# Two layers of a hybrid DeltaNet, sliding-window and memory-attention trunk: decay differences from two split passes with a triangle of ones, and two attention steps each one unit later

## The chip, the cores and the metric

The kernel runs on one core of a Trainium2 chip. The metric is device time in microseconds of one execution, the median of several. PE is the TensorE matmul engine, PEld its weight loads, DVE VectorE, ACT ScalarE, POOL GpSimd, SP the queue that issues the weight DMAs.

## The reference, cut to what matters

```python
def hybrid_layer(x, mem_n, ...):
    h = layer_norm(ALPHA * x + 0.5 * swiglu(x, ...))
    (dn_q, dn_k, dn_v, dn_b, dn_a, dn_z, sw_q, sw_k, sw_v, xa_q, gates) = split(h @ w_in)
    o_dn = deltanet_branch(dn_q, dn_k, dn_v, dn_b, dn_a, dn_z, ...)
    o_sw = sliding_window_attention(sw_q, sw_k, sw_v, swa_sinks)
    o_xa = memory_cross_attention(xa_q, mem_n, w_mem_kv)
    merged = sum_n sigmoid(gates_n) * (branch_n @ w_branch_n)
    h = layer_norm(ALPHA * h + merged @ w_out)
    return layer_norm(ALPHA * h + 0.5 * swiglu(h, ...))
```

In the DeltaNet branch g is a log-decay per token and head, and the scores are weighted with the decay between two tokens:

```python
g = cumsum(g)
decay = exp(where(tril, g[..., :, None] - g[..., None, :], NEG_INF))
```

The difference of the two running sums is the sum of g over the tokens after the earlier and up to the later one. There are 256 tokens, two layers, four DeltaNet heads of 128, eight window heads of 64 with a window of 128 tokens and two key/value heads, four memory heads of 128. Everything is float32.

## The kernel before, in words

**Weights** stream from DRAM in one array, in the order of use, as *units* of 128 x 1024 numbers (`unit`, line 103). Each unit is loaded by SP into `raw` (four buffers), cast to `whi` on ACT (a rounded float32, the type that PE takes in one pass), and the rest `raw - whi` goes to `wlo` on DVE (both in `split`, line 125). `whi` and `wlo` have five buffers each, so the cast of a unit waits until PE has read the unit five before it. A float32 product is made of three such matmuls (`mm3`: high x high, high x low, low x high). A matmul of two plain float32 operands is left to PE, which then runs several passes; the trace shows each as two records.

**PSUM** has four banks `acc` for the projections and two each of `at` (attentions) and `sm` (DeltaNet). A bank is handed on in turn, so its next writer waits until all readers of its last content are done.

**Order of the work.** `mixers` (once for each layer) runs the projections of the three branches as a stream of units. `weave` hangs small steps of the attentions and of the DeltaNet behind given units. The instructions of PE stay in program order there (`pinned`). On ACT, DVE and POOL a scheduler chooses the order when the program is built; the queue of each engine then runs in that fixed order, whatever is ready.

The steps that matter here, with their lines:

- `spread(c)` (line 652), for the two blocks c of 128 tokens: POOL has made `TM[c][:,0]`, the triangle `mlt` times g for four heads (line 673); PE multiplies each head's 128 x 128 block with the triangle `tri`, all plain float32, into one `sm` bank; DVE adds the mask (L658), ACT takes the exponential (L659).
- `gates(n)` projects the gates of branch n in eight units; each unit is twelve matmuls of 512 columns, and a tanh (L977) follows the fourth and the eighth. `gates(1)` carries the steps that are moved.
- `w_scores(tb, hh)` makes window scores of 128 tokens and half of the heads: six matmuls into two `at` banks, L736 on DVE (scale and mask), L742 to L746 (maximum), L745 and L748 on ACT (four exponentials), L749 and L750 on DVE, and L751 on ACT, four scalings by one over the sum. `w_turn` transposes the result on PE; ACT and DVE copy it (L761). `w_values(tb)` multiplies it with the values and splits the result.
- `double()` is the next stage of the inversion of two triangular matrices (one for each c), seven stages in all: small matmuls into `sm` for c=0 and then for c=1, and copies back. The copies of stage three are L856, two for each c, all four on ACT.

Of the kernel before, what the change touches and what calls it, by code (L numbers as in the profile page):

```python
# [11 lines left out]
F32R = mybir.dt.float32r  # L12
I32 = mybir.dt.int32
AF = mybir.ActivationFunctionType
ALU = mybir.AluOpType
AX = mybir.AxisListType

P = 128
# [20 lines left out]
def tile_trunk(ctx, tc, x, xT, mem, memT_, wst, lnp, memln, cvw, rows, cst, out):  # L39
    nc = tc.nc  # L40
# [3 lines left out]
    pc = ctx.enter_context(tc.tile_pool(name="pc", bufs=1))  # L44
    praw = ctx.enter_context(tc.tile_pool(name="praw", bufs=4))
    pu = ctx.enter_context(tc.tile_pool(name="pu", bufs=1))
    p2 = ctx.enter_context(tc.tile_pool(name="p2", bufs=2))
# [7 lines left out]
    def nm(s):  # L55
        uid[0] += 1
        return f"{s}_{uid[0]}"
# [4 lines left out]
    def T(pool, shape, tag, dt=F32, bufs=None):  # L62
        pool = pn if pool is pu and tag in NEAR else pool
        kw = {} if bufs is None else {"bufs": bufs}
        return pool.tile(shape, dt, tag=tag, name=nm(tag), **kw)
# [4 lines left out]
    def at():  # L70
        return T(psT, [P, 512], "at")

    def sm():
        return T(psS, [P, 512], "sm")
# [7 lines left out]
    tri = cs[:, C_TRI:C_TRI + P]  # L82
    mlt = cs[:, C_LT:C_LT + P]
    dtm = cs[:, C_DTM:C_DTM + P]

    def over4(ap):
        return ap.unsqueeze(1).to_broadcast([P, 4, ap.shape[-1]])
# [36 lines left out]
    def split(hi, lo, src):  # L124
        return nc.scalar.copy(hi, src).ins, nc.vector.tensor_tensor(lo, src, hi.bitcast(F32), op=ALU.subtract).ins  # L125
# [3 lines left out]
    def pe(ins):  # L129

        return tc.keep_in_program_order(ins) if pinned[0] else ins

    def matmul(*a, **k):
        return pe(nc.tensor.matmul(*a, **k))  # L134
# [10 lines left out]
    def weave(work, steps):  # L145

        for n, _ in enumerate(work, 1):
            for f in steps.get(n, ()):
                f()

    def projB(xt, nt, kpu, behind=None):
        g = projB_parts(xt, nt, kpu, behind)
        while True:
            try:
                next(g)
            except StopIteration as e:
                return e.value

    def projB_parts(xt, nt, kpu, behind=None):
        banks = [acc().rearrange("p (t s) -> p t s", t=2) for _ in range((nt + 1) // 2)]  # L160
        for uu in range(KD // kpu):
            hi, lo = unit(behind=behind)
            for kk in range(kpu):
                k = uu * kpu + kk
                for t in range(nt):
                    c = (kk * nt + t) * P
                    o = banks[t // 2][:, t % 2, :]
                    lastt = t % 2 == 1 or t == nt - 1
                    matmul(o, hi[:, c:c + P], xt[0](k), start=(k == 0 and t % 2 == 0), stop=False, skip_group_check=True)
                    matmul(o, hi[:, c:c + P], xt[1](k), start=False, stop=False, skip_group_check=True)  # L170
                    matmul(o, lo[:, c:c + P], xt[0](k), start=False, stop=(k == KD - 1 and lastt), skip_group_check=True)
            yield
        return banks

    def halves(xt, use):

        for i in range(2):
            (b,) = yield from projB_parts(xt, 2, 4)
            use(i, b)
# [66 lines left out]
    def acc_of(t):  # L246
        return (lambda k: t[0][:, k, :], lambda k: t[1][:, k, :])
# [271 lines left out]
    def mixers(l, hT, mkT, mv_, post):  # L519
        xt = acc_of(hT)  # L520
# [79 lines left out]
        def col(tag):  # L600
            return T(pu, sh, tag)
# [30 lines left out]
        g = col("g")  # L632
# [15 lines left out]
        TM = [T(pu, [P, 2, 4, P], f"w{2 + c}") for c in range(2)]  # L648
        AK = [T(pu, [P, 4, 2, P], f"u{12 + c}") for c in range(2)]
        hb = lambda ap: ap.unsqueeze(2).to_broadcast([P, 4, P])  # L650

        def spread(c):

            gm, dt = TM[c][:, 0], TM[c][:, 1]
            ps = sm().rearrange("p (h c) -> p h c", h=4)
            for h in range(4):
                matmul(ps[:, h, :], gm[:, h, :], tri, start=True, stop=True)
            nc.vector.tensor_tensor(dt, ps, over4(dtm), op=ALU.add)  # L658
            nc.scalar.activation(dt, dt, AF.Exp)  # L659

        def products(c, hh):
# [6 lines left out]
            for j in range(2):  # L668
                h = 2 * hh + j
                nc.vector.scalar_tensor_tensor(AK[c][:, h], TM[c][:, 1][:, h, :].unsqueeze(1).to_broadcast([P, 2, P]), cS[:, c, h:h + 1], ps[:, j], op0=ALU.mult, op1=ALU.mult)  # L670

        for c in range(2):
            nc.gpsimd.tensor_tensor(TM[c][:, 0], over4(mlt), hb(g[:, c, :]), op=ALU.mult)


        xq = (T(pu, [P, 4, S], "u4", F32R), T(pu, [P, 4, S], "u6", F32R))
# [47 lines left out]
        def w_scores(tb, hh):  # L724

            ts = slice(tb * P, (tb + 1) * P)
            nk = P if tb == 0 else 2 * P
            msk = cs[:, C_SW + P:C_SW + 2 * P] if tb == 0 else cs[:, C_SW:C_SW + 2 * P]
            pr = wpr[tb, hh] = T(p2, [P, 4, S], "pp")
            for j in range(0, 2, 2 * P // nk):  # L730

                nj = 2 * P // nk
                ps = at().rearrange("p (j v k) -> p j v k", j=nj, v=2)
                for i in range(nj):
                    mm3(ps[:, i], [t[:, 2 * hh + j + i, ts] for t in sq_], [t[:, :, 0:nk] for t in swk], True, True)
                nc.vector.scalar_tensor_tensor(pr[:, 2 * j:2 * j + 2 * nj, :nk], ps.rearrange("p j v k -> p (j v) k"), 0.125, msk.unsqueeze(1).to_broadcast([P, 2 * nj, nk]), op0=ALU.mult, op1=ALU.add)  # L736
            mxs = T(p3, [P, 2, 2], "mx")
            sums = T(p3, [P, 4], "sums")
            sk = T(p3, [P, 2, 2], "sk")
            sink = sinks[:, 2 * hh:2 * hh + 2, :]  # L740
            flat = lambda t: t.rearrange("p i v -> p (i v)")
            nc.vector.tensor_reduce(flat(mxs), pr[:, :, :nk], axis=AX.X, op=ALU.max)  # L742
            nc.vector.tensor_tensor(mxs, mxs, sink, op=ALU.max)
            nc.vector.tensor_tensor(sk, sink, mxs, op=ALU.subtract)
            nc.scalar.activation(flat(sk), flat(sk), AF.Exp)  # L745
            nc.vector.tensor_scalar(flat(mxs), flat(mxs), -1.0, None, ALU.mult)  # L746
            for h in range(4):
                nc.scalar.activation(pr[:, h, :nk], pr[:, h, :nk], AF.Exp, bias=mxs[:, h // 2, h % 2:h % 2 + 1], accum_out=sums[:, h:h + 1])  # L748
            nc.vector.tensor_tensor(sums, sums, flat(sk), op=ALU.add)  # L749
            wpr["end"] = nc.vector.reciprocal(sums, sums).ins  # L750
            [nc.scalar.mul(pr[:, h, :nk], pr[:, h, :nk], sums[:, h:h + 1]) for h in range(4)]  # L751
# [11 lines left out]
        def w_values(tb):  # L763
            if not oS:
                oS.extend(T(pu, [P, 4, S], tag, F32R) for tag in ("u6", "u7"))
            ts = slice(tb * P, (tb + 1) * P)
            pso = at()
            for kb in range(tb + 1):
                for kv in range(2):
                    hs = slice(kv * 64, kv * 64 + 64)  # L770
                    matmul(pso[hs, :], swv[:, kb, hs], wpT[tb][kb][:, kv].rearrange("p h q -> p (h q)"), start=kb == 0, stop=kb == tb)
            split(oS[0][:, :, ts], oS[1][:, :, ts], pso.rearrange("p (h k) -> p h k", h=4))
# [43 lines left out]
        def use_sq(i, b):  # L816
            split(*(t[:, 2 * i:2 * i + 2, :] for t in sq_), b)

        weave(halves(xt, use_xq), {3: [tok_v]})
        (b,) = projB(xt, 1, 8)  # L820
        for kv in range(2):
            hs = slice(kv * 64, kv * 64 + 64)
# [157 lines left out]
        def branch(n, o):  # L980
# [27 lines left out]
            3: [lambda: w_turn(0, 1), begin_inverse],  # L1008
            4: [lambda: w_scores(1, 0)]})
        weave(gates(1), {  # L1010
            1: [lambda: w_values(0), double],
            2: [lambda: w_scores(1, 1)],
            3: [double],
            5: [double, lambda: w_turn(1, 0)],
            6: [double, lambda: w_turn(1, 1)],
            7: [double, lambda: w_values(1)],
# [56 lines left out]
    ps = sm()  # L1073
# [14 lines left out]
    for l in range(NL):  # L1088
        mT = []
        mid = memory_T(mT, l)  # L1090
        if l == 0:

            mid[2] = lambda: load(cs, cst)
            more = {4: lambda *a: xres(0), 6: lambda *a: xres(1), 8: lambda *a: small()}
        post = Post(lnp[l, 0, 0], lnp[l, 0, 1])
        f1.rest(hT, 4, [((pu, "u0"), (pu, "u1")), ((pu, "u2"), (pu, "u3"))], post, mid, ends, {} if l else more)
        kv = memory_kv(mT, post.end)
        if l == 0:
            nc.scalar.activation(nea, rw[:, :, 8:12], AF.Exp)
            nc.vector.tensor_scalar(nea, nea, -1.0, None, ALU.mult)  # L1100
        post2 = Post(lnp[l, 1, 0], lnp[l, 1, 1])
        mixers(l, post.hT, *kv, post2)
        f2 = Ffn()
        begin(f2, post2.hT)
        last = l == NL - 1
        post = Post(lnp[l, 2, 0], lnp[l, 2, 1], last)
        f2.rest(post2.hT, 6, [((pu, a), (pu, b)) for a, b in (("u0", "u1"), ("u2", "u3"), ("u4", "u5"), ("u6", "u13"))], post, behind=post2.end)
        ends = post.end
        if not last:
            f1, hT = Ffn(), post.hT  # L1110
            begin(f1, hT)
# [87 lines left out]
```

## Time and profile before

| | |
|---|---|
| median of 3 runs | 1274.8 us (1273.62 to 1275.08) |
| profiled execution, its own time | 1273.52 us |
| its span | 1271.7 us |
| PE busy | 1261.0 us (99%) |
| DVE / ACT / POOL busy | 865.5 / 660.7 / 206.7 us (68 / 52 / 16%) |
| mean granted TensorE clock | 0.999 |

The profiled execution's own time is 1.8 us over its span, and 1.3 us under the median. A PE that is busy 99% says that it always has a matmul under way by the profile, not that each runs at its best: ends of matmuls are modelled, and a matmul that starts late shows first in the distance from one start to the next.

### The profile page before, as it was taken

How to read it: one execution, taken by the hardware profiler on the slowest of the kernel's cores; microseconds unless marked ns; L12 is line 12 of the kernel's file. 1: busy time of each engine (PE TensorE's matmuls, PEld its weight loads, DVE VectorE, ACT ScalarE, POOL GpSimd, SP SyncE). 2: the span in 40 equal slices, each digit the busy share in tenths (PEclk: the TensorE clock that was granted, in tenths of full speed). 3: DMA queues.
4: the chain of work that ended last, by engine and by line, in shares of the span. 5: the costliest groups of instructions: out<-in, count | busy, mean ns of one | idle time of the engine just before them, and what ended most of it. 6: DMA issues, size and time to landing. Idle time of an engine off the chain costs nothing.

```text
span 1271.7 us, 18766 instructions
## 1 busy us (share of the span) xinstructions
PE 1261.0 (99%) x6948; PEld 1073.7 (84%) x6948; DVE 865.5 (68%) x1273; ACT 660.7 (52%) x982; POOL 206.7 (16%) x365
## 2 busy tenths in 40 slices
PE   9999999999999999999999999999999999999997
PEld 6888889999878888888888888899987788888886
DVE  6678576897647776665766665759867388666555
ACT  6456444655664544454454554456556554444441
POOL 1232100002311102221012220000023101122200
PEclk9999999999999999999999999999999999999999
DMA  8988765655534748786667886566464356577762
GB/s 301 307 272 281 256 212 158 206 170 134 173 117 145 243 142 257 240 242 220 216 208 245 256 256 214 180 185 212 151 167 134 100 188 226 174 245 245 241 223 81
DMA packets 77499, 261.40 MB, mean 206 GB/s; under 512 B 11904, under 2 KB 13056, under 8 KB 77408
## 3 DMA queue, kind: packets, MB, share of 16 engines
q1 hardware_dynamic: 66320, 232.53, 55.8%
q0 software_dynamic: 11088, 27.68, 8.0%
q8 instruction: 54, 0.88, 0.3%
q14 instruction: 37, 0.30, 0.1%
HBM read 246.40 MB, written 13.76 MB: 205 GB/s over the span
## 4 chain that ended last, share of the span: by engine, by line
PE 96%; DVE 1%; DMA 1%; ACT 1%; issue 0%; SPq 0%; DVEq 0%; ACTq 0%
PE acc L134 85%; PE at L134 4%; PE sm L134 3%; PE sm L137 2%; DMA raw<-in_wst_dram 1%; DVE wlo L125 1%; PE acc L328 1%; PE acc L329 1%; PE acc L331 1%; PE at L137 1%; ACT whi L125 1%; DVE h L291 0%; DVE pp L736 0%; DVE w L940 0%; SPq L115 0%
## 5 line engine op out<-in xcount | busy, mean ns | idle before, releaser
L125 DVE TENSOR_TENSOR wlo<-raw,whi 128x1024 fp32r<-128x1024 f32 (+2 forms) x405 | 489.0, 1214 | 280.1 <-ACT whi L125 277.5
L125 ACT CAST whi<-raw 128x1024 fp32r<-128x1024 f32 (+2 forms) x405 | 413.6, 1029 | 400.1 <-PE acc L134 321.2
L134 PE MATMUL acc<-whi,hT 128*128 128x512 f32 (+1 forms) x1824 | 563.0, 386 | 0.4 <-ACT whi L125 0.4
L134 PEld LDWEIGHTS acc<-whi,hT 128*128 128x128 f32 x1824 | 340.2, 188 | 70.0 <-ACT whi L125 2.1
L134 PE MATMUL acc<-wlo,hT 128*128 128x512 f32 (+1 forms) x912 | 350.3, 384 | 0.0
L134 PE MATMUL acc<-whi,u 128*128 128x512 f32 x812 | 259.7, 392 | 0.0
L134 PEld LDWEIGHTS acc<-wlo,hT 128*128 128x128 f32 x912 | 171.4, 188 | 32.9 <-DVE wlo L125 1.1
L134 PEld LDWEIGHTS acc<-whi,u 128*128 128x128 f32 x812 | 152.3, 188 | 32.2 <-DVE u L125 0.5
L134 PE MATMUL acc<-wlo,u 128*128 128x512 f32 x406 | 158.2, 390 | 0.0
L358 POOL DMA_DIRECT2D tr<-t x176 | 96.2, 553 | 307.9 <-DVE t L352 299.3
L134 PE MATMUL acc<-hT,whi 128*128 128x256 f32 x672 | 122.3, 284 | 0.0
L134 PEld LDWEIGHTS acc<-hT,whi 128*128 128x128 f32 x672 | 104.7, 192 | 0.0
L134 PE MATMUL acc<-hT,wlo 128*128 128x256 f32 x336 | 95.1, 283 | 0.0
L134 PEld LDWEIGHTS acc<-wlo,u 128*128 128x128 f32 x406 | 76.3, 188 | 15.3
L134 PEld LDWEIGHTS acc<-hT,wlo 128*128 128x128 f32 x336 | 64.3, 192 | 0.0
L359 POOL DMA_DIRECT2D pt<-tr x44 | 25.0, 568 | 196.9 <-DMA tr<-t 128.9
L349 ACT ACTIVATE t<-acc 128x256 f32<-128x256 f32 x88 | 33.4, 379 | 36.7 <-PE acc L134 36.6
L134 PE MATMUL acc<-u,u 128*128 128x512 f32 x186 | 46.4, 394 | 0.0
L350 DVE TENSOR_TENSOR t<-t,acc 128x256 f32<-128x256 f32 x88 | 36.6, 416 | 8.0 <-ACT t L349 4.7
L995 POOL TENSOR_TENSOR u<-u,gt 128x512 f32<-128x512 f32 x16 | 20.7, 1294 | 125.0 <-DVE gt L993 125.0
L134 PEld LDWEIGHTS acc<-u,u 128*128 128x128 f32 x186 | 34.6, 188 | 7.5
L125 DVE TENSOR_TENSOR u<-pt,u 128x512 fp32r<-128x512 f32 x44 | 28.9, 657 | 10.3 <-ACT u L125 10.3
(236 smaller groups left out, 1163.7 us busy)
## 6 DMA issues: line engine op xcount, KB each, us to landing
raw<-in_wst_dram SPq DMA_DIRECT2D x409, 512.0 KB, 4.4
tr<-t POOLq DMA_DIRECT2D x176, 64.0 KB, 4.0
pt<-tr POOLq DMA_DIRECT2D x44, 256.0 KB, 5.2
raw<-in_wst_dram SPq DMA_DIRECT2D x16, 324.0 KB, 3.0
gB<-in_lnp_dram SPq DMA_DIRECT2D x6, 512.0 KB, 5.9
bB<-in_lnp_dram SPq DMA_DIRECT2D x6, 512.0 KB, 6.2
w<-dr POOLq DMA_DIRECT2D x4, 512.0 KB, 11.2
t<-in_xT_dram SPq DMA_DIRECT2D x4, 256.0 KB, 5.5
```

Source lines behind the costliest of these rows:

```text
L125: return nc.scalar.copy(hi, src).ins, nc.vector.tensor_tensor(lo, src, hi.bitcast(F32), op=ALU.subtract).ins
L134: return pe(nc.tensor.matmul(*a, **k))
L137: return pe(nc.tensor.transpose(*a))
L328: nc.tensor.matmul(ps, hT[0][:, k, ts], hi[:, c], start=k == 0, stop=False)
L329: nc.tensor.matmul(ps, hT[0][:, k, ts], lo[:, c], start=False, stop=False)
L331: nc.tensor.matmul(ps, hT[1][:, k, ts], hi[:, c], start=False, stop=k == KD - 1)
L349: act = nc.scalar.activation(t[:, :, tb, :], g, AF.Silu).ins
L350: ins = nc.vector.tensor_tensor(t[:, :, tb, :], t[:, :, tb, :], u, op=ALU.mult).ins
L358: nc.gpsimd.dma_start(d[:, :, q].rearrange("b c x -> c b x"), z[32 * q:32 * q + 32].rearrange("c (b x) -> c b x", b=4))
L359: back = nc.gpsimd.dma_start(y, d.rearrange("b c q x -> (b c) (q x)")).ins
L995: nc.gpsimd.tensor_tensor(mg[tb][:, js], mg[tb][:, js], gt[tb][:, js], op=ALU.add)
```

## The change

1. `spread` works with a new constant `later`, the triangle `mlt` cast to the rounded type (exact, it holds ones and zeros), as the stationary operand. The moving operand is now `tri` times g, made by POOL as before and split into a high and a low part by the new `spread_parts` (a cast on ACT and a subtraction on DVE of 128 x 512 for each c) into a tile of the pool that later holds the gates' tanh. Two matmuls of 512 columns, high and low, replace the four plain float32 ones.
2. `spread_parts(0)` and `spread_parts(1)` hang behind the first and third unit of the memory queries' projection.
3. In `gates(1)`, `w_values(0)` goes from behind unit 1 to behind unit 2, and `w_scores(1, 1)` from behind unit 2 to behind unit 3.

```diff
+    later = pc.tile([P, P], F32R, name="later")
...
         def spread(c):
-            gm, dt = TM[c][:, 0], TM[c][:, 1]
+            dt = TM[c][:, 1]
             ps = sm().rearrange("p (h c) -> p h c", h=4)
-            for h in range(4):
-                matmul(ps[:, h, :], gm[:, h, :], tri, start=True, stop=True)
+            for n in range(2):
+                matmul(ps, later, gms[c][n], start=n == 0, stop=n == 1)
...
+        gms = {}
         for c in range(2):
-            nc.gpsimd.tensor_tensor(TM[c][:, 0], over4(mlt), hb(g[:, c, :]), op=ALU.mult)
+            nc.gpsimd.tensor_tensor(TM[c][:, 0], over4(tri), hb(g[:, c, :]), op=ALU.mult)
+
+        def spread_parts(c):
+            both = T(p2, [P, 2, 4, P], "gt", F32R)
+            gms[c] = both[:, 0], both[:, 1]
+            split(*gms[c], TM[c][:, 0])
...
-        weave(halves(xt, use_xq), {3: [tok_v]})
+        weave(halves(xt, use_xq), {1: [lambda: spread_parts(0)], 3: [tok_v, lambda: spread_parts(1)]})
...
         weave(gates(1), {
-            1: [lambda: w_values(0), double],
-            2: [lambda: w_scores(1, 1)],
-            3: [double],
+            1: [double],
+            2: [lambda: w_values(0)],
+            3: [double, lambda: w_scores(1, 1)],
             5: [double, lambda: w_turn(1, 0)],
             6: [double, lambda: w_turn(1, 1)],
...
+            nc.scalar.copy(later, mlt)
             nc.scalar.activation(nea, rw[:, :, 8:12], AF.Exp)
```

New lines shift the numbers of the code behind them: L125 of before is L126 in the order of the change, L134 is L135, L745 to L751 are L753 to L759, L856 is L864, L871 is L879, L977 is L985.

**ACT, behind units 4 to 6 of `gates(1)`, layer 0, before.** The first cast needs the end of unit 4 on PE, the second of unit 5, the third of unit 6; `pp` are the window scores (1, 1), the first `w` copies fill the matrices of stage three.

```order
L745 ACTIVATE sk_3546<-sk_3546 128x4
L125 CAST whi_3828<-raw_3827 128x1024
L748 ACTIVATE pp_3533,sums_3545<-pp_3533,mx_3544 128x256 x4
L125 CAST whi_3834<-raw_3833 128x1024
L751 ACTIVATE pp_3533<-pp_3533,sums_3545 128x256 x4
L977 ACTIVATE gt_3451<-acc_3453 128x512
L856 COPY w_461_2590<-sm_3658 32x4x32 x2
L856 COPY w_462_2591<-sm_3669 32x4x32 x2
L761 COPY pt_3680<-at_3682 128x2x2x128
L125 CAST whi_3840<-raw_3839 128x1024
```

The same place in the changed program:

```order
L126 CAST whi_3832<-raw_3831 128x1024
L985 ACTIVATE gt_3455<-acc_3457 128x512
L126 CAST whi_3838<-raw_3837 128x1024
L753 ACTIVATE sk_3606<-sk_3606 128x4
L756 ACTIVATE pp_3593,sums_3605<-pp_3593,mx_3604 128x256 x4
L864 COPY w_461_2592<-sm_3662 32x4x32 x2
L864 COPY w_462_2593<-sm_3673 32x4x32
L759 ACTIVATE pp_3593<-pp_3593,sums_3605 128x256 x2
L126 CAST whi_3844<-raw_3843 128x1024
L759 ACTIVATE pp_3593<-pp_3593,sums_3605 128x256 x2
L864 COPY w_462_2593<-sm_3673 32x4x32
L769 COPY pt_3684<-at_3686 128x2x2x128
```

The exponentials moved from ahead of the second cast to behind it, and the third cast (`whi_3840`, now `whi_3844`) moved from behind all of this to the middle: two scalings, the fourth copy of stage three and the copy of `w_turn(1, 0)` now stand behind it. Layer 1 has the same two sequences.

**PE, behind units 1 to 3 of `gates(1)`, layer 0, before**, without the projection's own rows: the values (`at` from `pt`), stage one, the scores (1, 1) (`at` from `swk`, the last row of six), stage two.

```order
L134 MATMUL at_3474<-pt_3379,swv_2063 64x512 x2
L134 MATMUL sm_3479<-w_470_2601,l_469_2600 32x32 x16
L134 MATMUL sm_3497<-w_470_2601,l_469_2600 32x32 x16
...
L134 MATMUL at_3539<-swk_99,bB_2599 128x512
...
L134 MATMUL sm_3580<-w_470_2601,w_461_2590 32x32 x16
L134 MATMUL sm_3599<-w_470_2601,w_462_2591 32x32 x16
```

The same in the changed program:

```order
L135 MATMUL sm_3476<-w_470_2603,l_469_2602 32x32 x16
L135 MATMUL sm_3494<-w_470_2603,l_469_2602 32x32 x16
...
L135 MATMUL at_3532<-pt_3383,swv_2065 64x512 x2
...
L135 MATMUL sm_3555<-w_470_2603,w_461_2592 32x32 x16
L135 MATMUL sm_3574<-w_470_2603,w_462_2593 32x32 x16
...
L135 MATMUL at_3599<-swk_100,bB_2601 128x512
```

The values stand alone behind unit 2, and the scores follow stage two directly; stages one and two stay behind units 1 and 3.

## Rows read from the trace of the kernel before

**Rows 1.** The page, busy time of each engine.
```profile
PE 1261.0 (99%) x6948; PEld 1073.7 (84%) x6948; DVE 865.5 (68%) x1273; ACT 660.7 (52%) x982; POOL 206.7 (16%) x365
```
**Rows 2.** Timeline of PE around both spreads (start, us, engine, line, operation, count).
```profile
283.62 0.28 PE L134 MATMUL acc<-hT,wlo 128*128 128x256 f32 x1
...
283.75 1.05 PE L134 MATMUL sm<-cs,w 128*128 128x128 f32 x8
...
284.55 1.66 PE L134 MATMUL at<-u,u 128*128 128x256 f32 x12
...
286.05 0.40 PE L134 MATMUL acc<-hT,whi 128*128 128x256 f32 x2
...
288.81 0.28 PE L134 MATMUL acc<-hT,wlo 128*128 128x256 f32 x1
...
290.06 0.29 PE L134 MATMUL acc<-hT,wlo 128*128 128x256 f32 x1
```
**Rows 3.** Timeline of PE, end of unit 1 of `gates(1)` and the steps behind it.
```profile
341.90 0.39 PE L134 MATMUL acc<-wlo,hT 128*128 128x512 f32 x1
...
342.13 0.39 PE L134 MATMUL acc<-whi,hT 128*128 128x512 f32 x1
...
342.70 1.08 PE L134 MATMUL at<-pt,swv 128*64 128x512 f32 x4 [0.18 <-DVE pp L736]
...
343.70 1.51 PE L134 MATMUL sm<-w,l 32*32 32x32 f32 x64
...
345.14 0.50 PE L134 MATMUL acc<-whi,hT 128*128 128x512 f32 x1
```
**Rows 4.** Timeline of PE, stage two behind unit 3.
```profile
351.94 0.39 PE L134 MATMUL acc<-whi,hT 128*128 128x512 f32 x1
...
352.26 1.51 PE L134 MATMUL sm<-w,w 32*32 32x32 f32 x64
...
353.69 0.50 PE L134 MATMUL acc<-whi,hT 128*128 128x512 f32 x1
```
**Rows 5.** Timeline of PE, last matmuls of units 5 and 6, stage four, `w_turn(1, 1)`.
```profile
359.04 0.39 PE L134 MATMUL acc<-whi,hT 128*128 128x512 f32 x1
...
363.63 0.39 PE L134 MATMUL acc<-whi,hT 128*128 128x512 f32 x1
363.95 0.89 PE L134 MATMUL sm<-w,w 32*32 32x32 f32 x32
364.77 1.09 PE L137 MATMUL at<-cs,pp 128*128 128x128 f32 x8
```
**Rows 6.** Timeline of ACT, the same stretch.
```profile
356.37 0.20 ACT L745 ACTIVATE sk<-sk 128x4 f32<-128x4 f32 x1
...
357.70 0.51 ACT L748 ACTIVATE pp<-pp,mx 128x256 f32<-128x256 f32 x1
...
359.68 1.03 ACT L125 CAST whi<-raw 128x1024 fp32r<-128x1024 f32 x1
360.61 1.71 ACT L751 ACTIVATE pp<-pp,sums 128x256 f32<-128x256 f32 x4
362.22 0.58 ACT L977 ACTIVATE gt<-acc 128x512 f32<-128x512 f32 x1
362.81 1.08 ACT L856 COPY w<-sm 32x128 f32<-32x128 f32 x4
363.92 0.58 ACT L761 COPY pt<-at 128x512 f32<-128x512 f32 x1
```
**Rows 7.** Timeline of PE and ACT, end of unit 7 and the cast that waits for it.
```profile
368.23 0.39 PE L134 MATMUL acc<-whi,hT 128*128 128x512 f32 x1
...
368.65 1.04 ACT L125 CAST whi<-raw 128x1024 fp32r<-128x1024 f32 x1 [0.64 <-PE acc L134]
```
**Rows 8.** The last stretch of the span (busy us of PE, PEld, DVE, ACT, POOL, then PEclk).
```profile
1265.00:1271.00 6.00, 0.00 (x0) 0.00 (x0) 3.25 (x8) 0.21 (x1) 0.00 (x0) 0.83 0.23 87
```
**Rows 9.** Timeline of DVE, the mask of the second spread.
```profile
290.02 0.69 DVE L658 TENSOR_TENSOR w<-sm,cs 128x512 f32<-128x512 f32 x1 [1.43 <-PE sm L134]
```

## The prediction

> **What bounds the kernel now.** I read the page first: PE is busy 99% of the span [rows 1], so almost every microsecond taken from PE's stream, or added to it, reaches the end, and work on ACT, DVE or POOL counts only where PE waits for it. As a late start hides in the modelled ends, I then read the timeline at the places that change, by distances between starts. A step of 256 columns takes 0.12 us (twelve in the 1.50 us from 284.55 to 286.05 [rows 2]), one of 512 columns 0.23 us (341.90 to 342.13 [rows 3]). Then I looked for who waits on whom among PE and ACT in `gates(1)`, since ACT's order is what moves most there [rows 5 to 7]. The casts of units stand behind PE: the one behind unit 7 begins 0.03 us after that unit's last matmul ends (368.23 + 0.39 = 368.62, cast at 368.65 [rows 7]). So all five buffers are full, and a cast is some four units ahead of its use.
>
> **Removed from PE: the plain float32 spreads.** The last projection matmul before the first spread starts at 283.62, the one after the spread and the twelve of the memory scores at 286.05: 2.43 us [rows 2]. Now: 0.12 to the spread, two passes of 0.23, twelve of 0.12 to 0.125, together 2.02 to 2.08. The saving is about 0.4. At the second spread 288.81 to 290.06 is 1.25 [rows 2]; now 0.12 + 0.46 + two steps of 0.12, 0.82; the saving is 0.43. There are two of each over the layers: 1.65 us, say 1.7. Bounds: the block of eight records alone lasts 0.80 (283.75 to 284.55 [rows 2]), which leaves 0.34 a spread and 1.4 in all, if nothing is saved at its edges; 2.1 if the edges give 0.1 more each.
>
> **Added for it.** For each c a cast and a subtraction of half a unit's columns, and once the cast of `later`. They lie on ACT and DVE beside PE's projections. Before the second spread's mask DVE sits idle 1.43 us [rows 9], about the two subtractions, so the delay has died down there; the casts of weights have their lead of four units, 4 x 2.8 us. POOL's product with `tri` has the same shape as that with `mlt`. The early cast of `later` waits for the constants' DMA in the first feed-forward and holds the casts behind it; the same lead covers that. I cost all of this at nothing. If the cover were gone, one late cast (1.03 [rows 6]) and a subtraction, taken as long, would stand on the path, 2.1 us a layer.
>
> **The values a unit later.** Before, PE went from unit 1 to the values (0.57 us after the last start, where stage two begins 0.32 after its unit [rows 3, 4]; so 0.25 was a wait for L736), needed 1.00 for them, then stage one: 342.13 to 345.14, 3.01. Stage two alone, with entry, takes 351.94 to 353.69, 1.75 [rows 4]. Sum 4.76. Now: stage one alone, 1.75; the values alone, 0.32 + 1.00; stage two, 1.75; less the 0.23 of the one more projection step in between, plus some 0.1 for one more slow step after a change of shape: 4.7. The wait goes, but a change of shape comes. Gain 0.06 a layer, 0.1 in all; bounds 0 and 0.5 (the whole waits).
>
> **The scores (1, 1) a unit later: a new wait on ACT.** This is the term that decides. ACT now runs the cast that needs unit 5 *before* the four exponentials, and puts the cast that needs unit 6 *before* the last two scalings, the fourth copy of stage three and the copy of `w_turn(1, 0)`, as the order shows. Stage four for c=1 on PE writes the `sm` bank that this fourth copy reads, and `w_turn(1, 1)` writes the `at` bank that the other copy reads. Both stand on PE directly behind unit 6. So PE must wait for a chain that begins with its own last matmul of that unit. In the times of before:
>
> - Unit 5 ends at 359.04 + 0.39 = 359.43 [rows 5], the cast starts at 359.46, and what follows it may start 0.93 later (359.68 to 360.61 [rows 6]): 360.39.
> - The small exponential 0.20, four exponentials 1.98 (357.70 to 359.68), three copies of 0.28 (four in 1.11, 362.81 to 363.92), two scalings of 0.40 (four in 1.61, 360.61 to 362.22) [rows 6]: 364.21.
> - Unit 6 ends at 364.02 [rows 5], so its cast is free by then: 364.21 to 365.14; two scalings, 365.95; the fourth copy 0.27, 366.22; the copy of `w_turn`, 0.28 behind its start, from 366.23, lasts 0.58 to 366.81.
> - Stage four for c=1 starts at about 366.3, where it was at 364.36 (half of 0.82 after 363.95); `w_turn(1, 1)` at about 366.85, where it was at 364.77 [rows 5].
>
> PE loses 2.1 us a layer. Before, there was no room here either: the last copy ended at 363.89 and stage four began at 363.95 [rows 5, 6], so nothing cushions it. Layer 1 has the same order: 4.2 us in all. Lower bound: if ACT reaches the cast in time, 364.05 + 0.93 + 0.80 + 0.27 + 0.06 puts stage four at 366.1, 1.75 a layer, 3.5 in all. Upper bound: 3.0 a layer, if the maxima of the scores reach ACT about a cast's length late. I take the middle chain, as every link has a row. Queued behind it: unit 7, stage five and everything after it shift with PE; their casts and copies are then early, so nothing else waits.
>
> **Sum.** -1.7 - 0.1 + 4.2 = +2.4 us, on the profiled execution 1273.5 to 1275.9. That execution lies 1.3 under the median shown; carried to the median 1274.8, the forecast is **1277.2 us**. A difference under 0.2%, 2.55 us, is about what a measurement of this kernel cannot tell from none, and the forecast stands just inside it: its terms span +1.4 to +3.6.
>
> **Rivals.**
>
> - *The scores' maxima come late, and the wait is longer: slower.* The scores now start on PE at about 352.2, DVE then has a unit's subtraction, two products of the branch, the mask, the reduction and another subtraction, some 7 us in sequence by their durations, an estimate of 359.8 for the small exponential's operand, against 360.39 on ACT. From 0.6 us of slip on, each further one is PE's loss. For it: DVE kept PE waiting for L736 in this very stretch [rows 3]. Against: part of DVE's work there is done earlier now. At 1 us a layer: +4.4, 1279.2. Chance 0.11.
> - *PE does not have to wait there*, because the banks are handed on differently from what I read: then the gains alone, -1.8, 1273.0. Against: the 0.06 us between the fourth copy and stage four. Chance 0.09.
> - *PE's clock falls in the gap: slower.* The gap leaves PE about 2 us with nothing between the halves of stage four. In the last 6 us of the span PE has no matmul, and its granted clock is 0.83 in the mean [rows 8]: two levels, 1.00 and 0.50, make that some 4 us at the upper one, so a gap of 2 us should keep 2.4 GHz. If it fell, a unit of twelve steps (2.8 us) would take twice as long: +2.8 a layer, 1282.8. [...] Chance 0.04.
> - *The change does not do what it says*: the two passes run at the pace of plain float32. The values' four such records of 512 columns take 1.00 [rows 3]; the spread would then save nothing, +4.1, 1278.9. Or the cover of the added casts fails, +2.1 a layer. Together chance 0.04.
>
> **How the numbers follow.** The forecast has 0.72. Its span and the spread of the runs (0.7 us either way) put about 0.42 of it inside 2.55 us, 0.27 above, and 0.03 below for a gain that I don't see. The late maxima, the clock and the last rival are slower, 0.11 + 0.04 + 0.04. No wait gives 0.07 inside and 0.02 below. So faster 0.05, same 0.49, slower 0.46. The range 1275.0 to 1279.6 takes the forecast's terms with the runs' spread and the late maxima, and leaves out no wait, the clock and the last rival, not quite 2 in 10.
>
> **What would show it.** Right: two records of 512 columns in the spread and about 0.46 us for them; the values behind unit 2 without a wait for L736; PE waiting for the copy L864 and the copy L769 behind unit 6 in both layers, some 2 us, with the cast just ahead of the scalings on ACT; a clock of 1.00 throughout. Wrong: stage four for c=1 within 0.5 us of c=0; a wait of the spread on its split; a weight cast on which PE waits; waits at other places of the chain.

## The result, and the profile after

| | before | after |
|---|---|---|
| median | 1275.0 us (9 runs, 1273.62 to 1278.74) | 1279.39 us (9 runs, 1275.70 to 1282.78) |
| profiled execution, its span | 1273.52, 1271.7 us | 1280.43, 1278.7 us |
| PE busy | 1261.0 us [rows 1] | 1263.2 us |
| mean granted TensorE clock | 0.999 | 0.996 |

After over before is 1.0032, 95% interval [1.0019, 1.0045]: about 4 us slower, with the whole interval above 1. The forecast was 1277.2; the time lies in the range, at its upper end. The runs of the change also scatter more, over 7 us. In the table of the experiments one run of e10, 2104.62 us at a mean clock of 0.556, is left out as slow.

The page of the change, busy time of each engine, against [rows 1]:

```profile
PE 1263.2 (99%) x6924; PEld 1074.1 (84%) x6924; DVE 867.5 (68%) x1277; ACT 662.0 (52%) x987; POOL 206.4 (16%) x365
```

The share of PE says nothing: 99% before and after. The list of what PE waited for (us in total, times, longest) says more:

```profile
PE sm L135 <- ACT w L864: 3.8, 2, 1.9
...
PE sm L135 <- DVE w L948: 1.3, 2, 1.1
```

The first line is new, one wait in each layer. Of the second, 1.1 us is in layer 1 of this execution alone: in the kernel before and in all twelve kernels below this line kept PE waiting at most 0.2 at a time, so I take it as chance (a load of weights landed in 4.96 us there instead of 3.4). The wait for L736 of before [rows 3] (now L744) is gone.

**The spreads.** PE in the change, both spreads of layer 0 (start, us, engine, line, operation, count), against [rows 2]:

```profile
283.89 0.28 PE L135 MATMUL acc<-hT,wlo 128*128 128x256 f32 x1
284.01 0.62 PE L135 MATMUL sm<-gt,later 128*128 128x512 f32 x2
...
285.89 0.40 PE L135 MATMUL acc<-hT,whi 128*128 128x256 f32 x2
...
288.64 0.28 PE L135 MATMUL acc<-hT,wlo 128*128 128x256 f32 x1
288.76 0.62 PE L135 MATMUL sm<-gt,later 128*128 128x512 f32 x2
...
289.45 0.28 PE L135 MATMUL acc<-hT,wlo 128*128 128x256 f32 x1
```

From 283.89 to 285.89 is 2.00, against 2.43 before; from 288.64 to 289.45 is 0.81, against 1.25. Each spread saves 0.43 to 0.44.

**The wait.** PE behind unit 6, layer 0, against [rows 5]:

```profile
362.93 0.39 PE L135 MATMUL acc<-whi,hT 128*128 128x512 f32 x1
363.25 0.59 PE L135 MATMUL sm<-w,w 32*32 32x32 f32 x16
365.72 0.59 PE L135 MATMUL sm<-w,w 32*32 32x32 f32 x16 [1.88 <-ACT w L864]
366.33 1.30 PE L138 MATMUL at<-cs,pp 128*128 128x128 f32 x8
367.28 0.77 PE L135 MATMUL acc<-whi,hT 128*128 128x512 f32 x1
367.86 0.63 PE L135 MATMUL acc<-wlo,hT 128*128 128x512 f32 x1
...
371.38 0.39 PE L135 MATMUL acc<-whi,hT 128*128 128x512 f32 x1
```

ACT in the same stretch, against [rows 6]:

```profile
358.76 1.04 ACT L126 CAST whi<-raw 128x1024 fp32r<-128x1024 f32 x1 [1.17 <-PE acc L135]
...
361.92 0.81 ACT L864 COPY w<-sm 32x128 f32<-32x128 f32 x3
362.75 0.91 ACT L759 ACTIVATE pp<-pp,sums 128x256 f32<-128x256 f32 x2
363.56 1.03 ACT L126 CAST whi<-raw 128x1024 fp32r<-128x1024 f32 x1
364.50 0.90 ACT L759 ACTIVATE pp<-pp,sums 128x256 f32<-128x256 f32 x2
365.41 0.26 ACT L864 COPY w<-sm 32x128 f32<-32x128 f32 x1
```

The chain runs link by link as predicted. The first cast stands idle 1.17 us until PE has ended unit 5, with the four exponentials behind it; the second runs in the middle of the scalings; the fourth copy comes last. From the last matmul of unit 6 to `w_turn(1, 1)` PE needs 3.40 (362.93 to 366.33), against 1.14 before (363.63 to 364.77 [rows 5]). That is 2.26 us lost; layer 1 loses 2.25.

**The clock.** In windows of 2 us the change shows this (us, PE busy, instructions, granted clock, DMA share, GB/s):

```profile
364.00:366.00 2.00, 0.28 (x12) 1.00 0.04 14
366.00:368.00 2.00, 1.98 (x23) 0.77 0.51 125
368.00:370.00 2.00, 2.00 (x7) 0.50 0.34 137
370.00:372.00 2.00, 2.00 (x16) 0.88 0.00 0
```

Behind the wait the clock fell to 0.50, the lower level (1.2 GHz), and came back to 2.4 GHz while PE worked throughout. It did not fall in the wait itself: it was 1.00 still from 366.0 to 367.0, with PE at work again since 365.72, and 0.54 in the mean from 367.0 to 368.0. At the lower level a step of 512 columns takes 0.42 (367.86 to 368.28) instead of 0.23. From `w_turn(1, 1)` to the last matmul of unit 7 is 5.05 us (366.33 to 371.38), against 3.46 before (364.77 [rows 5] to 368.23 [rows 7]): 1.6 more. Layer 1 shows the same, 1.55. The Trainium skill (TensorE: Matmul & The Clock Gate, section HAM oscillation — how this bites in real kernels) tells of a kernel in which waits of some 3 to 5 us between bursts of matmuls put the engine back to the lower level each time. In this trace a wait of 1.88 us was enough, in both layers.

The 7.0 us between the two spans are thus 4.5 of waits, 3.15 of clock, 1.0 of L948 and about -1.7 of spreads; the small rest lies in different starts.

### The profile page after: what moved, and what is told of

The parts are those of the page before. It is cut to its first block, busy times and chain, and to the rows that moved or that the text cites. A ratio compares the mean times of both kernels' runs of the same rounds, so it can differ in the third digit from the quotient of the medians.

```text
span 1278.7 us, 18728 instructions
## 1 busy us (share of the span) xinstructions
PE 1263.2 (99%) x6924; PEld 1074.1 (84%) x6924; DVE 867.5 (68%) x1277; ACT 662.0 (52%) x987; POOL 206.4 (16%) x365
## 4 chain that ended last, share of the span: by engine, by line
PE 96%; ACT 1%; DMA 1%; DVE 1%; SPq 0%; issue 0%; DVEq 0%; ACTq 0%
PE acc L135 85%; PE at L135 4%; PE sm L135 2%; PE sm L138 2%; DMA raw<-in_wst_dram 1%; PE acc L329 1%; PE acc L330 1%; PE acc L332 1%; ACT whi L126 1%; PE at L138 1%; DVE wlo L126 0%; ACT pp L756 0%; ACT pp L759 0%; ACT w L864 0%; DVE h L292 0%
## 5 line engine op out<-in xcount | busy, mean ns | idle before, releaser
L126 DVE TENSOR_TENSOR wlo<-raw,whi 128x1024 fp32r<-128x1024 f32 (+2 forms) x405 | 486.6, 1209 | 296.2 <-ACT whi L126 293.6
L126 ACT CAST whi<-raw 128x1024 fp32r<-128x1024 f32 (+2 forms) x405 | 413.5, 1029 | 400.6 <-PE acc L135 319.9
L135 PE MATMUL acc<-whi,hT 128*128 128x512 f32 (+1 forms) x1824 | 564.4, 387 | 0.5 <-ACT whi L126 0.5
L135 PEld LDWEIGHTS acc<-whi,hT 128*128 128x128 f32 x1824 | 341.3, 189 | 72.0 <-ACT whi L126 2.4
L135 PE MATMUL acc<-wlo,hT 128*128 128x512 f32 (+1 forms) x912 | 351.1, 385 | 0.2 <-DVE wlo L126 0.2
L135 PE MATMUL acc<-whi,u 128*128 128x512 f32 x812 | 259.6, 392 | 0.0
L135 PEld LDWEIGHTS acc<-wlo,hT 128*128 128x128 f32 x912 | 172.0, 189 | 33.4 <-DVE wlo L126 1.3
L135 PEld LDWEIGHTS acc<-whi,u 128*128 128x128 f32 x812 | 152.3, 188 | 32.1 <-DVE u L126 0.5
L135 PE MATMUL acc<-wlo,u 128*128 128x512 f32 x406 | 158.2, 390 | 0.0
L135 PE MATMUL acc<-hT,whi 128*128 128x256 f32 x672 | 122.1, 284 | 0.0
L135 PEld LDWEIGHTS acc<-hT,whi 128*128 128x128 f32 x672 | 104.8, 192 | 0.2
L135 PE MATMUL acc<-hT,wlo 128*128 128x256 f32 x336 | 95.0, 283 | 0.0
L135 PEld LDWEIGHTS acc<-wlo,u 128*128 128x128 f32 x406 | 76.3, 188 | 15.3
L135 PEld LDWEIGHTS acc<-hT,wlo 128*128 128x128 f32 x336 | 64.4, 192 | 0.0
L135 PE MATMUL acc<-u,u 128*128 128x512 f32 x186 | 46.4, 394 | 0.0
L135 PEld LDWEIGHTS acc<-u,u 128*128 128x128 f32 x186 | 34.6, 188 | 7.5
L549 DVE SCALAR_TENSOR_TENSOR t<-acc,cw,t 128x255 f32<-128x255 f32 (+2 forms) x72 | 34.5, 479 | 1.0
```

The source lines that it names most:

```text
L549: nc.vector.scalar_tensor_tensor(yc[:, j, d:], b[:, j, :S - d], w[:, t:t + 1], yc[:, j, d:], op0=ALU.mult, op1=ALU.add)
```

## The experiments

All ratios are to the kernel before, on the same chip, and come from the runs and not from the two medians. The waits are those of the profiled execution, summed over both layers.

| run | median us (range, runs) | ratio, 95% interval | wait for L744 | wait for L864 |
|---|---|---|---|---|
| the change | 1279.39 (1275.70 to 1282.78, 9) | 1.0032 [1.0019, 1.0045] | none | 3.8 |
| e1 spreads, no move | 1278.52 (1274.61 to 1280.49, 8) | 1.0028 [1.0016, 1.0039] | 2.6 | none |
| e2 moves, old spreads | 1278.21 (1277.85 to 1281.15, 5) | 1.0036 [1.0023, 1.0048] | none | 3.8 |
| e3 the change, ACT's order mended | 1273.09 (1272.84 to 1274.84, 11) | 0.9990 [0.9981, 0.9999] | none | none |
| e4 the change, gap filled | 1276.23 (1275.26 to 1277.98, 11) | 1.0013 [1.0004, 1.0022] | none | filled |
| e5 only the values moved | 1279.54 (1275.95 to 1283.36, 8) | 1.0041 [1.0026, 1.0056] | 3.3 | none |
| e6 only the scores moved | 1283.29 (1280.91 to 1284.58, 4) | 1.0066 [1.0053, 1.0079] | 3.7 | 3.8 |
| e7 e1, rest on POOL | 1276.16 (1274.05 to 1280.81, 11) | 1.0014 [1.0004, 1.0023] | 2.1 | none |
| e8 before, unused splits | 1280.63 (1278.02 to 1281.97, 5) | 1.0046 [1.0033, 1.0059] | 4.0 | none |
| e9 e3, rest on POOL | 1273.17 (1271.36 to 1274.35, 11) | 0.9987 [0.9979, 0.9996] | none | none |
| e10 only the second cast held | 1274.86 (1273.38 to 1277.11, 10) | 1.0008 [0.9998, 1.0017] | none | 1.9 |
| e11 gap half filled | 1276.47 (1275.76 to 1278.41, 11) | 1.0018 [1.0009, 1.0027] | none | 1.6 |
| e12 before, unused casts | 1280.59 (1278.15 to 1282.27, 6) | 1.0047 [1.0034, 1.0060] | 3.4 | none |

**e1: the spreads alone.** The table of steps in `gates(1)` is put back:

```diff
-            1: [double],
-            2: [lambda: w_values(0)],
-            3: [double, lambda: w_scores(1, 1)],
+            1: [lambda: w_values(0), double],
+            2: [lambda: w_scores(1, 1)],
+            3: [double],
```

> The two-pass spreads with the steps of gates(1) where they were before. Theory A (the loss is ACT's order behind units 4 to 6, which only the moves bring, and the clock's fall in the gap that follows): ACT's order there is the one of before, so no wait of some 2 us on PE, clock 1.00 in both layers, and only the spreads' gain: about -1.7 us, 1273.3 against 1275.0. Theory B (the added casts and subtractions for the spreads cost the time, by what they push back on ACT and DVE): the time stays near the change's, +3 to +4. Theory C (the gain of the spreads is given back elsewhere): within 0.5 us of before.

ACT's order behind units 4 to 6 was the one of before and the wait for L864 was absent, but the time did not fall: 1.0028. PE in layer 1 (start, us, and in brackets the idle time and who ended it):

```profile
974.01 1.98 PE L135 MATMUL at<-pt,swv 128*64 128x512 f32 x4 [2.47 <-DVE pp L744]
975.92 2.31 PE L135 MATMUL sm<-w,l 32*32 32x32 f32 x64
```

The values behind unit 1 wait 2.47 us for L744 in layer 1, where they waited 0.18 before (as in layer 0 [rows 3]); the clock then stands at 0.50 (the 64 small matmuls take 2.31 instead of 1.51). From the values to the last matmul of the next unit PE needs 7.94 us (974.01 to 981.95), against 5.11 before (972.18 to 977.29): this fall costs 2.8. Theory A was wrong on this point, and B, which I had not favoured, was near. What makes L744 late is followed up in e7, e8 and e12.

**e2: the moves alone.** The moved table stays; the old spread is put back, with POOL's old product, and nothing is split for it.

```diff
...
-            for n in range(2):
-                matmul(ps, later, gms[c][n], start=n == 0, stop=n == 1)
+            for h in range(4):
+                matmul(ps[:, h, :], gm[:, h, :], tri, start=True, stop=True)
...
```

> The plain float32 spreads of before, the two moves of gates(1) alone. Theory A: ACT's order is the change's, so PE waits some 2.25 us a layer for the fourth copy of stage three, and in executions in which the clock then falls another 1.6 a layer: +4.5 to +7.5 in the median, about 1280 to 1281, with the granted clock at 0.50 for some 3 us behind at least one of the two gaps. Theory B: no loss, 1274.5 to 1275.0. Theory C (the moves cost by the changed shapes on PE): +0.5 to +1.5.

Theory A in the wait, which is the change's, 1.88 us in each layer; 1.0036 is the low end of its +4.5 to +7.5 us, as in the profiled execution the clock held, against the expectation:

```profile
366.00 0.59 PE L134 MATMUL sm<-w,w 32*32 32x32 f32 x16 [1.88 <-ACT w L856]
366.61 1.09 PE L137 MATMUL at<-cs,pp 128*128 128x128 f32 x8
...
370.06 0.39 PE L134 MATMUL acc<-whi,hT 128*128 128x512 f32 x1
```

From `w_turn(1, 1)` to the end of unit 7 is 3.45 us (366.61 to 370.06), as before, and layer 1 is the same. So this gap can cost 2.25 us or 3.85; which one differs from execution to execution. Of the five runs four had a mean clock of 0.998 or 0.999, and the one at 0.995 took 1281.15. I found no rule for it.

**e3: the change with ACT's order mended.** `hold` is the ACT copy of `w_turn(1, 0)`, `exp` the last exponential of `w_scores`; `behind` makes the cast and the rest of a unit issue after it, and `issue_after` ties the copies of stage three to `exp`.

```diff
...
-            us = [unit() for _ in range(4)]
+            us = [unit(behind=wpr["hold"] if n == 1 and i in (1, 2) else None) for i in range(4)]
...
-            for e, o in pairs:
-                nc.scalar.copy(M[o, :, e], ps[o])
+            with tc.issue_after(wpr["exp"]):
+                for e, o in pairs:
+                    nc.scalar.copy(M[o, :, e], ps[o])
```

> The whole change, with the casts that need units 5 and 6 held on ACT behind the copy of w_turn(1, 0), so that exponentials, scalings and copies of stage three run first. Theory A: stage four for c=1 follows c=0 within 0.5 us, w_turn(1, 1) waits 0 to 0.4, clock 1.00 in both layers, -1.0 to -1.9 us: 1273.1 to 1274.0. Theory B (the moves cost wherever ACT runs its casts, as the scores come late): PE still loses 1 us a layer or more there, 1275.5 or above. Rival to the mend itself: the two held casts are late for their units and PE waits for a weight, a wait for whi or wlo in branch(1) of some 1 us.

ACT now runs (layer 0):

```profile
358.89 0.20 ACT L753 ACTIVATE sk<-sk 128x4 f32<-128x4 f32 x1 [1.07 <-DVE sk L752]
...
361.20 0.81 ACT L868 COPY w<-sm 32x128 f32<-32x128 f32 x3
362.02 1.71 ACT L760 ACTIVATE pp<-pp,sums 128x256 f32<-128x256 f32 x4
363.74 0.26 ACT L868 COPY w<-sm 32x128 f32<-32x128 f32 x1
364.02 0.59 ACT L770 COPY pt<-at 128x512 f32<-128x512 f32 x1
364.51 2.00 ACT L126 CAST whi<-raw 128x1024 fp32r<-128x1024 f32 x2
```

and PE:

```profile
363.48 1.16 PE L135 MATMUL sm<-w,w 32*32 32x32 f32 x32
364.66 1.09 PE L138 MATMUL at<-cs,pp 128*128 128x128 f32 x8
```

Stage four is one piece again, and `w_turn(1, 1)` begins 1.18 behind it, against 0.82 before (363.95 to 364.77 [rows 5]): 0.36 of the loss is left. The two casts now begin at 364.51, one behind the other, where the change had them at 358.76 and 363.56, and no matmul waits for them. 1273.09 us, ratio 0.9990, with the interval just below 1: the change as it is meant, without its queue. It is faster than both kernels, by about 1.3 us than before and by 5 to 6 than the change.

**e4 and e11: PE kept at work in the gap.** Behind the first half of stage four come matmuls into columns of its `sm` bank that nothing reads:

```diff
-            ps = part()
+            bank = sm()
+            ps = bank[:, 0:P].rearrange("p (h c) -> p h c", h=4)
...
+            for _ in range(0 if c else 10):
+                matmul(bank[:, P:], later, swk[0].rearrange("p v k -> p (v k)")[:, P:], start=True, stop=True, skip_group_check=True)
```

> The change, with ten matmuls of 384 columns, whose result nothing reads, between the two halves of stage four on PE, so that PE works in the gap; ACT's order is the change's, and the wait for the fourth copy stays where it was in time. Theory A (the clock falls because PE stands idle): the granted clock stays at 1.00 through both layers, w_turn(1, 1) starts as late as in the change or up to 0.3 later, and from it to the last projection matmul of unit 7 takes 3.4 to 3.5 instead of 5.0: the median comes down by 1.5 to 3.2, to about 1276.5 to 1278. Theory B (the clock falls for another reason, the small matmuls of stage four or the load of the engines): 0.50 stays behind the gap, 1279.5 to 1280.5.

PE in e4, layer 0:

```profile
362.94 0.59 PE L135 MATMUL sm<-w,w 32*32 32x32 f32 x16
363.46 2.02 PE L135 MATMUL sm<-swk,later 128*128 128x384 f32 x10
365.42 0.59 PE L135 MATMUL sm<-w,w 32*32 32x32 f32 x16
366.03 1.09 PE L138 MATMUL at<-cs,pp 128*128 128x128 f32 x8
...
369.48 0.39 PE L135 MATMUL acc<-whi,hT 128*128 128x512 f32 x1
```

The second half of stage four starts 2.48 behind the first, as late as in the change (2.47), but unit 7 ends 3.45 us after `w_turn(1, 1)` begins, not 5.05. The windows of e4 (the columns as above):

```profile
366.00:368.00 2.00, 1.98 (x14) 1.00 0.64 172
368.00:370.00 2.00, 2.00 (x15) 1.00 0.22 90
```

Twenty useless matmuls make the program faster: 1.0013 against 1.0032. All eleven runs have a mean clock of 0.998 or 0.999, where the change has 0.994 to 0.999. The small matmuls and the load are still there, so here the fall needs PE to be idle; that idleness is not enough for it, e2 shows. What is left over e3 is mostly the wait.

> As e4, with five matmuls of 384 columns in the gap instead of ten, so that PE works about half of it. If any work in the gap that leaves under a microsecond of it idle keeps the clock: 1.00 throughout and the median of e4, 1276.0 to 1276.6, as the start of w_turn(1, 1) is set by ACT. If the clock still falls in some executions: 1277 to 1279, with a spread like the change's.

With five of them PE is idle 0.81 us, and the clock held in the profiled execution. The median is nearly e4's, but three of the eleven runs took 1277.9 to 1278.4, two of them at mean clocks of 0.996 and 0.997, so I do not claim that it always holds.

**e10: which of the two casts.** As e3, but only the cast that needs unit 6 is held, without the tie to `exp`:

```diff
...
-            us = [unit() for _ in range(4)]
+            us = [unit(behind=wpr["hold"] if n == 1 and i in (2,) else None) for i in range(4)]
```

> The change with only the cast that needs unit 6 held behind the copy of w_turn(1, 0); the cast that needs unit 5 stays ahead of the four exponentials. By the chain of the change's own times: exponentials end at 361.8, three copies and four scalings at 364.3, the fourth copy at 364.5, the copy of w_turn(1, 0) at 365.1, while stage four's first half starts at 363.25: PE loses 0.8 to 1.1 a layer instead of 2.25, no fall of the clock seen so far behind gaps under 1 us: 1274.4 to 1275.5. Rival (the second cast is the whole of the loss): 1273.0 to 1273.5; (the first is): 1276 or more.

```profile
357.73 1.04 ACT L126 CAST whi<-raw 128x1024 fp32r<-128x1024 f32 x1 [1.17 <-PE acc L135]
...
363.42 0.26 ACT L866 COPY w<-sm 32x128 f32<-32x128 f32 x1
```

PE waits 0.93 in each layer, and from the last matmul of unit 6 to `w_turn(1, 1)` it needs 2.44 (361.90 to 364.34), a loss of 1.30 a layer: somewhat more than the 0.8 to 1.1 expected. The median is 1274.86, as expected. Each of the two casts carries a part of the 1.88.

**e5 and e6: one move at a time**, both with the new spreads. In e5 the values are behind unit 2 with the scores directly behind them; in e6 the scores go behind unit 3 and the values stay behind unit 1. The table of e5, and then that of e6:

```diff
-            1: [double],
-            2: [lambda: w_values(0)],
-            3: [double, lambda: w_scores(1, 1)],
+            1: [double],
+            2: [lambda: w_values(0), lambda: w_scores(1, 1)],
+            3: [double],
```

```diff
-            1: [double],
-            2: [lambda: w_values(0)],
+            1: [lambda: w_values(0), double],
             3: [double, lambda: w_scores(1, 1)],
```

> The two-pass spreads and the values behind unit 2; the scores (1, 1) stay behind unit 2 as before, and ACT's order behind units 4 to 6 is the one of before. If the moved scores alone bring ACT's order and its wait, and the moved values alone cover the late L744: no wait for L864, none for L744 above 0.3, clock 1.00, 1272.6 to 1273.6, as with the mended order (1273.1). Rival: the values' move brings a loss of its own (the change of shape at the extra stop, the scores directly behind the values), 1274.5 or more.

A miss: 1.0041 instead of a gain. ACT's order behind units 4 to 6 is good there and the values do not wait, but the scores do, 2.12 us in layer 0 and 1.20 in layer 1. DVE and then PE of e5, layer 0:

```profile
348.17 1.23 DVE L126 TENSOR_TENSOR wlo<-raw,whi 128x1024 fp32r<-128x1024 f32 x1 [1.60 <-ACT whi L126]
349.31 0.68 DVE L744 SCALAR_TENSOR_TENSOR pp<-at,cs 128x512 f32<-128x512 f32 x1
```

```profile
346.96 0.73 PE L135 MATMUL at<-swk,u 128*128 128x512 f32 x2
350.05 0.73 PE L135 MATMUL at<-swk,u 128*128 128x512 f32 x2 [2.12 <-DVE pp L744]
```

Values and scores together want three turns of the two `at` banks at once. The second half of the scores waits until L744 has read the first, and L744 stands on DVE behind the rest of a unit whose cast is late. The rival ("a loss of its own") held, by another way than I gave.

> The two-pass spreads and the scores (1, 1) behind unit 3; the values stay behind unit 1. ACT's order is the change's, DVE's the spread's: if the two waits are independent, both appear: about 1.9 for L864 in each layer and 2 to 2.5 for L744 in layer 1, with the clock at 0.50 behind two or three gaps: 1281 to 1285. Rival: the wait for L744 makes room for the casts on ACT, and the second wait shrinks, 1278 to 1280.

1.0066: the first case in size, but not in every place. L864 kept PE waiting 1.88 in each layer; the wait for L744 was long in layer 0 and not, as expected, in layer 1. PE in layers 0 and 1:

```profile
344.21 1.08 PE L135 MATMUL at<-pt,swv 128*64 128x512 f32 x4 [2.64 <-DVE pp L744]
...
975.93 1.08 PE L135 MATMUL at<-pt,swv 128*64 128x512 f32 x4 [1.04 <-DVE pp L744]
```

The clock held behind both gaps of layer 0, the one of 2.64 us too, and fell behind both of layer 1 (0.50 from 979 to 981 and from 1003 to 1004), the one of 1.04 us too. So the length of a gap does not tell here whether the clock falls.

The three pieces of the change therefore need one another. The new spreads make L744 late for the values; the values' move hides that; and the scores must then move out of the values' way.

**e7, e8 and e12: why L744 is late in e1.** The gather of the triangular blocks (two DMAs), POOL's fifteen steps on it and a transpose on DVE stand ahead of L744. Four weight subtractions of 4.59 us stand between that transpose and L744 in e1, as they did before (4.63). In e7, otherwise e1, the subtractions of the spread's split go to POOL:

```diff
-            split(*gms[c], TM[c][:, 0])
+            nc.scalar.copy(hi, TM[c][:, 0])
+            nc.gpsimd.tensor_tensor(lo, TM[c][:, 0], hi.bitcast(F32), op=ALU.subtract)
```

e8 is the kernel before with the whole splits of the change made and unused; in e12 only the casts are left of them:

```diff
-            split(*gms[c], TM[c][:, 0])
+            nc.scalar.copy(both[:, 0], TM[c][:, 0])
```

> As e1 (two-pass spreads, no move), with the two subtractions of the spread's split on POOL, which was idle there, so that DVE's order is word for word that of before. If it is DVE's 1.7 us of added work in front of the products of the branch that makes the gather, POOL's fifteen steps and L744 late in layer 1: the products on DVE end where they were before (L792 of layer 1 near 933.4 to 934.4, not 935.6), the wait for L744 falls from 2.5 to below 1.3, mostly without the clock's fall: median 1273.2 to 1275.0. Rival: the wait comes from PE being early and the gather landing late (13.1 instead of 11.1 in e1): it stays at 2 or more, 1277.5 to 1279.

Between the two cases, so the reason given is at most a part. With DVE's order that of before, L744 still kept PE waiting 0.59 and 1.52 us. DVE itself waits earlier, 2.65 us at the window keys, for ACT's cast of them.

> The kernel before, with the casts and subtractions for the spread made in the same places as in the change but read by nothing; the spreads stay plain float32, no step is moved. PE is not early here, DVE has the added 1.7 us. If DVE's added work is the cause: the wait for L744 in layer 1 grows from 0.2 to between 1 and 2, and in some executions the clock falls behind it: 1275.5 to 1278. Rival (PE's 0.85 us of earliness and the gather's landing are what count): no change, 1274.5 to 1275.2.

Unused work alone costs 0.46%, more than I expected: 4.0 us of waits, and the clock at 0.50 behind the one of layer 0.

> The kernel before, with the two casts of the spread's split on ACT alone (no subtraction), read by nothing; DVE's order is word for word that of before, ACT's differs by these casts and the one of the triangle. In e7 ACT stood 1.9 and 0.4 us waiting for POOL's products before them, and DVE's split of the window keys waited 2.65 for ACT. If these casts alone hold up the products of the branch and with them the gather: L744 keeps PE waiting 1.5 to 2.3 in both layers, as in e8, and the clock falls in most executions: 1277.5 to 1281. If DVE's subtractions were the cause after all: 1274.3 to 1275.3 and a wait of 0.2 to 0.4 a layer.

The casts alone (with the one of `later`) cost as much as the whole splits. ACT of before, and then of e12, layer 0:

```profile
278.58 0.36 ACT L125 CAST swk<-acc 64x256 fp32r<-64x256 f32 x1
281.18 0.37 ACT L125 CAST swk<-acc 64x256 fp32r<-64x256 f32 x1 [2.24 <-DVE swk L125]
```

```profile
278.75 0.36 ACT L126 CAST swk<-acc 64x256 fp32r<-64x256 f32 x1
281.04 0.62 ACT L680 CAST gt<-w 128x512 fp32r<-128x512 f32 x1 [1.92 <-POOL w L675]
282.04 0.62 ACT L680 CAST gt<-w 128x512 fp32r<-128x512 f32 x1 [0.38 <-POOL w L675]
282.68 0.37 ACT L126 CAST swk<-acc 64x256 fp32r<-64x256 f32 x1
```

ACT stands 2.3 us waiting for POOL's two products, as it also does in the change. The second cast of the keys starts 3.93 behind the first instead of 2.60, and the weight casts stand behind it. DVE's queue waits for these, and the last step on the branch's products ends 27.1 us behind the first cast of the keys (304.80 + 1.06 less 278.75), against 26.4 before (303.90 + 1.07 less 278.58). From there the gather carries the delay to L744. Its own landing varies besides, from 8.2 to 13.9 us over all profiled executions; I found no rule for it, and it decides how much of the delay PE sees. In e1, layer 1, the gather is issued 1.36 us later than before (941.49 against 940.13) and POOL waits 12.22 for it instead of 10.23, so that L744 starts 1.83 later (973.27 against 971.44). How the lateness divides between the casts and the landing is not separated by these runs; that the casts bring it, e8 and e12 show.

**e9: the mended version with the subtractions on POOL.** The edits of e3 and of e7 together.

> As e3 (the whole change with the two casts held), with the two subtractions of the spread's split on POOL as in e7. If e3 has no wait left that the change brings, and its values a unit later already cover the late L744: the same as e3, 1272.9 to 1273.3. Rival: part of DVE's added work still costs e3 something, and it goes: 1272.0 to 1272.8.

0.9987 against e3's 0.9990: nothing that could be told apart. Once the values stand behind unit 2, the late L744 costs nothing.

## Why the prediction was right, and where it was not

- **Spreads.** Right: 0.43 to 0.44 each, predicted 0.41 and 0.43.
- **The new wait on ACT.** Right in place, cause and size: 2.25 us a layer, predicted 2.1. Every link has its row, e2 shows that the moves alone bring it, e3 that the order and not the later scores is the cause, e10 that each cast carries a part. The lower bound, 1.75, took ACT to be at the second cast when unit 6 ends. It came there 0.24 late (363.56, against 362.93 + 0.39), as the first cast had waited 1.17 for PE; the middle chain had 0.19.
- **The late maxima**, a rival, fell: in the change DVE had written the operand of the small exponential by 358.62 (L752, 358.46 + 0.16), and ACT, busy with the cast, came to it at 359.72.
- **No wait**, a rival, fell with the same rows.
- **The clock**, a rival with 4 in 100, came true in both layers of the profiled execution and is the main error. The step that failed is the sentence on the end of the span: from a mean of 0.83 in [rows 8] I took it that PE could idle some 4 us at the upper level, so that a gap of 2 should keep it. The row was read short, too: PE's last matmul there had ended at 1263.67, and the clock was 1.00 until 1268.0 at least. But one idle stretch did not carry over to another: the gap of 1.88 did not keep the clock, in this execution, and did in e2's. The price was wrong the other way: 1.6 us a layer, not 2.8, as the clock was back before unit 7 had ended (in e1 a fall did cost 2.8). The runs' own clocks of 0.994 to 0.999 say that it falls in some executions and not in others, which fits the scatter of 7 us. Without it the sum, +2.4, would have been near e4's +1.7.
- **Added work at nothing.** Right for the change as a whole, wrong as reasoned. I looked at the lead of the weight casts and at DVE's idle time before the second spread's mask [rows 9]. What counts is that ACT, in order, waits for POOL's products, and that the delay does not die down at the mask but goes on to the gather. Its price if uncovered was put at 2.1 us a layer; e8 and e12 measured about 6 in all.
- **The values a unit later.** PE's steps came out as summed, but the term, 0.1, missed what the move is for. It removes not the 0.25 of before, but the 0.2 to 2.6 that the new casts would have made of it (e1, e6, e7).
- **The numbers.** "Same" and "slower" stood at 0.49 and 0.46, as the forecast lay on the border; the clock tipped it. That the time still lies in the range is in part luck: the range left the clock's fall out, and the fall cost 3.15 us in the profiled execution where its rival had 5.6.

## What to carry to other kernels

Where a scheduler fixes each engine's order, read the order of every in-order queue around a moved step, and look above all for an instruction that waits for the busiest engine standing ahead of one that releases a buffer to it: two such casts cost 4.5 us of waits here, and holding them back gave all but some 0.7 of it back. An added instruction is hidden only if what it waits for is early too, so follow the queue behind it to the next place where the bounding engine waits. And price a gap on TensorE with the clock in mind, as a cost that may or may not come.

## What was not expected of the hardware

- The clock fell to 0.50 behind a gap of 1.88 us in both layers of one program and held at 1.00 behind the same gap in both layers of another. In e6 it held behind 2.64 us and fell behind 1.04. Filling the gap with unread matmuls kept it.
- One gather of the same two DMAs landed in 8.2 to 13.9 us from its issue, in the fourteen profiled executions, for the same bytes.
